# A graph-attention kernel with a fixed issue order on all engines, blocks pipelined by hand, and row merges through 32x32 turns

## The chip, the cores and the metric

The kernel runs on one core of a Trainium2 chip. The core has a matmul engine (TensorE, PE in the profile, with its weight loads shown as PEld), a vector engine (VectorE, DVE), a scalar engine (ScalarE, ACT), a general engine (GpSimd, POOL) and an engine that mostly issues transfers (SyncE, SP). Each has its own queue and works through it in order; they meet at semaphores. Matrix products land in PSUM, a small memory of eight banks; everything else lies in SBUF or in device memory (DRAM). Transfers are issued by SP, ACT and POOL and carried by 16 shared DMA engines. The metric is the device time of one execution in microseconds (us).

## The reference

A graph has 4096 nodes with 64 features each and 50,000 edges (source, destination). Four heads project the nodes, every edge gets a weight from its two ends, and each node sums its weighted incoming messages and divides by the sum of the weights:

```python
for h in range(n_heads):
    x_proj[h] = x @ weight[h]
for h in range(n_heads):
    src_att = np.sum(x_proj[h, src_nodes] * att_src[h], axis=-1)
    dst_att = np.sum(x_proj[h, dst_nodes] * att_dst[h], axis=-1)
    edge_scores[h] = src_att + dst_att
edge_scores = np.where(edge_scores > 0, edge_scores, 0.2 * edge_scores)
for h in range(n_heads):
    for i in range(num_edges):
        output[h, dst_nodes[i]] += np.exp(edge_scores[h, i]) * x_proj[h, src_nodes[i]]
# then output[h, dst] /= (sum of exp(edge_scores) over the edges into dst) + 1e-8
```

The result is 4096 x 256 (four heads of 64) in float32.

## The kernel before, in words

**Two sorts bring the edges into blocks.** Each edge becomes one float32 key that holds source group, destination and source remainder (L283 to L286). The 50,000 keys lie as 128 rows of up to 391, padded to 512 columns. `Sorter.rows` sorts every row by a bitonic network of two-operand minimum and maximum instructions (`flip` at L163 and L165, `half` at L173; two instructions on 256 elements make a step). `Sorter.runs` then merges eight neighbouring rows into a run of 4096, in three rounds: a round exchanges keys with a partner row (a stream shuffle L188, a scaling L190 and a minimum L192, once, twice and three times in rounds one to three), rescales (L194) and does nine `half` steps. `store` (L200) writes the runs to DRAM. `below` (L208) counts on ACT, by sums of signs, how many keys lie under each boundary; `bounds` (L220 to L236) turns the counts into start and end of each window, with a matmul `cnt_ps` (L220) and a dozen small DVE instructions. `fetch` (L242, L244) gathers windows out of the stored runs with indirect transfers issued by POOL. The first sort groups edges by source; its windows, two of 256 keys in every row, are the rows of the second sort (`group`), which skips the row phases that are done already and orders by destination. Its windows (five of 128 keys) are unpacked (L339 to L346) into 16-bit node numbers and written to the DRAM table `gat_bins`.

**Between the sorts' inputs and the blocks lie the tables.** `xf` (x itself, loaded at L294) is cast to bf16 into `xa` (L316), transposed on PE (L322) into `xT`, and 66 small float32 matmuls `at_ps` (L327) give the two attention terms of every node. They need `uv`, made from `wS` (the weights, L296) and `attbd` (the attention vectors).

**34 blocks of 121 destination nodes do the work.** A block has 16 tiles of 128 edges. Its node numbers are loaded to all partitions at once (`bc`, 1 MB, L363, SP and POOL taking turns). DVE makes one-hot matrices from them (`oh`, L366 and L367). PE gathers with them the source rows and scores of every edge (`xps`, 48 matmuls, L377 to L381), ACT takes the exponentials (`ex`, L384 and L385) and copies the rows out (`xs`, L386). PE also multiplies the destination one-hots by an identity to turn them (`sp`, L391) and ACT copies them out (`Sb`, L393). DVE forms the weights `wv` (L396) and the weighted rows `val` (L400); POOL copies the weights into the last four columns of `val` (L399). 16 matmuls of 260 columns scatter-add into `acc` (L405). `finish` then divides on DVE (L411 to L414), transposes `agg` on PE (L419), copies (`aT`, L420), projects with the block-diagonal weights (`pf`, L422), copies (`res`, L424) and stores (L426).

**The order.** A scheduler of the language decides the order of the instructions on each engine, and tiles with a number of buffers (`oh`: two, `bc`: three, `xps`: two of two banks, `sp`: two) decide how far ahead an engine may run.

Of the kernel before, what the change touches and what calls it, by code (L numbers as in the profile page):

```python
# [9 lines left out]
P = 128  # L10
ALPHA = 0.2
# [24 lines left out]
def kernel(ctx: ExitStack, tc: tile.TileContext, x: bass.AP, edge_index: bass.AP,  # L36
# [12 lines left out]
    XC = Din + H  # L49
# [15 lines left out]
    eD = cst.tile([P, EL, 2], I32)  # L65
    if rem:
        r0 = rem // 32 * 32
        V.memset(eS[r0:P, E0, :], N)
        V.memset(eD[r0:P, E0, :], 0)
    for t, k, eng in ((eS, 0, nc.sync), (eD, 1, nc.scalar)):  # L70
        eng.dma_start(out=t[:, 0:E0, :], in_=ei[k, 0:P * E0, :].rearrange("(p e) c -> p e c", p=P))
    for t, k, eng in ((eS, 0, nc.sync), (eD, 1, nc.scalar)):
        if rem:
            eng.dma_start(out=t[0:rem, E0, :], in_=ei[k, P * E0:E, :])
# [3 lines left out]
    G.iota(pidx[:], pattern=[[1, 1]], base=0, channel_multiplier=1)  # L78
    ident = cst.tile([P, P], F32)
    make_identity(nc, ident[:])  # L80
    io = cst.tile([P, P], I32)
    G.iota(io[:], pattern=[[1, P]], base=0, channel_multiplier=0)
    ioF = cst.tile([P, P], F32)
    V.tensor_copy(out=ioF[:], in_=io[:])
    pF = cst.tile([P, 2], F32)
    V.tensor_copy(out=pF[:, 0:1], in_=pidx[:])
    V.tensor_scalar(out=pF[:, 1:2], in0=pF[:, 0:1], scalar1=float(P), scalar2=None, op0=OP.add)

    sgi = cst.tile([P, 3], I32)
    sg = cst.tile([P, 3], F32)  # L90
    for j in range(3):
        V.tensor_scalar(out=sgi[:, j:j + 1], in0=pidx[:], scalar1=1 << j, scalar2=None, op0=OP.bitwise_and)
        V.tensor_scalar(out=sg[:, j:j + 1], in0=sgi[:, j:j + 1], scalar1=-2.0 / (1 << j), scalar2=1.0,
                        op0=OP.mult, op1=OP.add)
    sgg = cst.tile([P, 2], F32)
    V.tensor_tensor(out=sgg[:], in0=sg[:, 0:2], in1=sg[:, 1:3], op=OP.mult)
# [8 lines left out]

    p8 = bits("p8", 3, 15)
# [3 lines left out]
    m16 = cst.tile([P, 16], F32)  # L110
    V.tensor_scalar(out=m16[:], in0=ioF[:, 0:16], scalar1=p8[:, 0:1], scalar2=None, op0=OP.is_equal)
    m8 = cst.tile([P, 8], F32)
    V.tensor_scalar(out=m8[:], in0=ioF[:, 0:8], scalar1=p16[:, 0:1], scalar2=None, op0=OP.is_equal)

    sel1 = cst.tile([P, 2, P], F32)
    for i in range(2):
        V.tensor_scalar(out=sel1[:, i, :], in0=av(ioF[:], 8 * i, [0, 16], [1, 8]), scalar1=p8[:, 0:1], scalar2=None,
                        op0=OP.is_equal)
    sel2 = cst.tile([P, P], F32)
    V.tensor_scalar(out=sel2[:], in0=av(ioF[:], 0, [0, 8], [1, 16]), scalar1=p8[:, 0:1], scalar2=None,  # L120
                    op0=OP.is_equal)
    nb1 = cst.tile([P, NR + 1], F32)
    V.tensor_scalar(out=nb1[:], in0=ioF[:, 0:NR + 1], scalar1=-float(SG), scalar2=SG / 2, op0=OP.mult, op1=OP.add)
# [3 lines left out]
    V.tensor_scalar(out=nb2[:], in0=nb2[:], scalar1=0.5, scalar2=None, op0=OP.add)  # L127
    pad = cst.tile([1, W1], F32)
# [4 lines left out]
    S.copy(out=identb[:], in_=ident[:])  # L133

    xa = cst.tile([P, NB, XC], BF16)
    adb = cst.tile([P, ND, H], BF16)
# [8 lines left out]
    class Sorter:  # L145
# [13 lines left out]
        def flip(self, k):  # L159
            s, d = self.step()  # L160
            h = 1 << (k - 1)
            n = L >> k
# [5 lines left out]
        def half(self, j):  # L168
# [7 lines left out]
        def rows(self, first):  # L176
# [321 lines left out]
```

## Time and profile before

| | us |
|---|---|
| time, median of three runs | 451.8 (449.31 to 452.3) |
| profiled execution: time | 452.86 |
| profiled execution: span in the trace | 450.8 |
| last store issued | 442.7 |

| engine | busy us | instructions |
|---|---|---|
| PE | 252.3 | 3102 |
| DVE | 290.0 | 594 |
| ACT | 193.3 | 526 |
| POOL | 98.4 | 84 |

The execution falls into stretches. Up to 106 us the first sort runs on DVE; to 157 us the second; to 181 us the windows travel through DRAM; from 181 to 443 us run the 34 blocks. No engine is busy throughout, so the shares over the whole span say little: each stretch is read by itself, first by the busy time of the engines in it, then by what each engine waited for. A row of the groups by line gives the busy time and the mean of one instruction, then the idle time just before and who ended it. In a timeline row, the first two numbers are start and duration in us, and a wait stands in brackets.

### The profile page before, as it was taken

To read this page: it belongs to the slowest core of one execution; us is meant where nothing else is said; L and a number is where in the kernel's file an instruction comes from. 1 tells how busy PE (TensorE), PEld (TensorE's weight loads), DVE (VectorE), ACT (ScalarE), POOL (GpSimd) and SP (SyncE) were. 2 spreads that over 40 slices of the span, in tenths; PEclk is the share of its full clock that TensorE was granted. 3 is DMA by queue.
4 is the path that set the end of the run, shared out by engine and by line. 5 is a ranking of instruction groups with operands and counts; after the bars stand their busy time and mean duration, and the time that the engine had idled before them with its cause. 6 is when DMAs were issued, how large, how long until landed. Compare 5 with 4: busy or idle time off the path is not lost.

```text
span 450.8 us, 7963 instructions
## 1 busy us (share of the span) xinstructions
PE 252.3 (56%) x3102; PEld 212.0 (47%) x3102; DVE 290.0 (64%) x594; ACT 193.3 (43%) x526; POOL 98.4 (22%) x84
## 2 busy tenths in 40 slices
PE   0599900000000000669877887789788978797881
PEld 0388800000000000557666776667666766676660
DVE  4960199994899821755586658665876577656830
ACT  1823100000896000435556555655565556555560
POOL 6100000001000040131342124422442144314400
PEclk9999999999999999868899889998989898989897
DMA  7000000001000014923435453544345443533000
GB/s 170 7 1 0 0 0 0 1 0 37 10 0 1 7 45 151 345 95 127 182 124 201 135 183 121 201 148 166 138 178 176 140 160 155 199 117 105 23 26 17
DMA packets 13547, 43.87 MB, mean 97 GB/s; under 512 B 3308, under 2 KB 8492, under 8 KB 9148
## 3 DMA queue, kind: packets, MB, share of 16 engines
q1 hardware_dynamic: 9156, 24.16, 16.0%
q0 software_dynamic: 3152, 18.49, 11.1%
q10 hardware_dynamic: 1192, 0.63, 0.5%
q8 instruction: 26, 0.43, 0.4%
q14 instruction: 21, 0.17, 0.1%
HBM read 38.22 MB, written 5.05 MB: 96 GB/s over the span
## 4 chain that ended last, share of the span: by engine, by line
DVE 37%; PE 35%; ACT 12%; issue 6%; DMA 6%; POOL 1%; ACTq 1%; POOLq 0%; DVEq 0%; SPq 0%
PE acc L405 9%; PE sp L391 8%; DVE oh L366 7%; ACT junk L208 7%; PE at_ps L327 6%; DVE val L400 6%; PE pf L422 6%; DVE sB L173 5%; DVE sA L173 5%; DVE oh L367 3%; PE pf L419 2%; ACT aT L420 2%; DVE agg L414 2%; DMA bc<-gat_bins 2%; PE xps L377 2%
## 5 line engine op out<-in xcount | busy, mean ns | idle before, releaser
L393 ACT CAST Sb<-sp 128x512 bf16<-128x512 f32 x136 | 77.7, 591 | 46.8 <-PE sp L391 46.2
L366 DVE TENSOR_SCALAR oh<-bc,pF 128x4096 bf16<-128x4096 bf16 x34 | 43.7, 1286 | 83.1 <-PE sp L391 70.1
L405 PE MATMUL acc<-val,Sb 128*128 128x260 bf16 x544 | 88.8, 303 | 0.8 <-DVE val L400 0.8
L399 POOL COPY val<-wv 128x64 bf16<-128x64 bf16 x34 | 73.6, 2165 | 34.4 <-DVE wv L396 21.3
L400 DVE TENSOR_TENSOR val<-xs,wv 128x4096 bf16<-128x4096 bf16 x34 | 78.0, 2295 | 2.3 <-DVE wv L396 0.5
L377 PE MATMUL xps<-xa,oh 128*128 128x68 bf16 x544 | 60.2, 194 | 32.9 <-DVE oh L366 32.5
L377 PEld LDWEIGHTS <-oh 128*128 128x128 bf16 x544 | 50.2, 98 | 38.2 <-DVE oh L366 36.2
L379 PE MATMUL xps<-xa,oh 128*128 128x68 bf16 x544 | 56.9, 198 | 11.6 <-DVE oh L367 11.6
L391 PE MATMUL sp<-identb,oh 128*128 128x128 bf16 x544 | 59.4, 239 | 0.4 <-ACT res L424 0.2
L405 PEld LDWEIGHTS <-Sb 128*128 128x128 bf16 x544 | 54.1, 109 | 10.7 <-DVE val L400 0.9
L381 PE MATMUL xps<-adb,oh 128*128 128x4 bf16 x544 | 56.1, 167 | 0.0
L379 PEld LDWEIGHTS <-oh 128*128 128x128 bf16 x544 | 48.7, 96 | 15.0 <-DVE oh L367 14.8
L208 ACT ACTIVATE junk<-kr,nb 128x512 f32<-128x512 f32 x34 | 24.5, 722 | 60.8 <-DVE kr L265 59.8
L391 PEld LDWEIGHTS <-oh 128*128 128x128 bf16 x544 | 46.0, 108 | 9.8 <-issue 2.8
L381 PEld LDWEIGHTS <-oh 128*128 128x128 bf16 x544 | 50.3, 100 | 0.3
L220 PE MATMUL cnt_ps<-sgn,sel 128*128 128x17 f32 (+1 forms) x6 | 1.9, 398 | 80.9 <-ACT sgn L211 80.7
L363 POOL DMA_DIRECT2D bc<-gat_bins x17 | 9.2, 543 | 152.1 <-DVE wv L396 135.3
L384 ACT ACTIVATE ex<-xps 128x32 f32<-128x32 f32 x68 | 13.5, 199 | 67.4 <-PE xps L381 67.4
L386 ACT CAST xs<-xps 128x512 bf16<-128x512 f32 x68 | 40.3, 593 | 0.0
L220 PEld LDWEIGHTS cnt_ps<-sgn,sel 128*128 128x128 f32 x6 | 1.5, 310 | 81.3 <-ACT sgn L211 81.0
L173 DVE TENSOR_TENSOR sB<-sA 128x256 f32<-128x256 f32 x100 | 38.1, 422 | 1.5
L173 DVE TENSOR_TENSOR sA<-sB 128x256 f32<-128x256 f32 x96 | 36.6, 421 | 1.4
(119 smaller groups left out, 339.0 us busy)
## 6 DMA issues: line engine op xcount, KB each, us to landing
bc<-gat_bins SPq DMA_DIRECT2D x17, 1024.0 KB
bc<-gat_bins POOLq DMA_DIRECT2D x17, 1024.0 KB, 5.1
out_dram<-res SPq DMA_DIRECT2D x33, 121.0 KB
gat_sorted<-sA SPq DMA_DIRECT2D x2, 256.0 KB
eS<-in_edge_index_dram SPq DMA_DIRECT2D x1, 390.0 KB
eD<-in_edge_index_dram ACTq DMA_DIRECT2D x1, 390.0 KB
gat_bins<-tb SPq DMA_DIRECT2D x5, 32.0 KB
gat_bins<-tb ACTq DMA_DIRECT2D x5, 32.0 KB
```

The costliest lines, as they stand in the source:

```text
L173: V.tensor_tensor(out=av(d[:], o, [2 * h, n], [1, h]), in0=av(s[:], 0, [2 * h, n], [1, h]), in1=av(s[:], h, [2 * h, n], [1, h]), op=op)
L208: S.activation(out=junk[:], in_=v, func=ACTF.Sign, bias=nbnd[:, b:b + 1], scale=1.0, accum_out=sgn[:, b:b + 1])
L366: V.tensor_scalar(out=oh[:, 0:2, :], in0=bc[:], scalar1=pF[:, 0:1], scalar2=None, op0=OP.is_equal)
L377: T.matmul(out=o, lhsT=oh[:, 1, e], rhs=xa[:, 2 * t, :], start=(i % 4 == 0), stop=False, skip_group_check=True)
L379: T.matmul(out=o, lhsT=oh[:, 2, e], rhs=xa[:, 2 * t + 1, :], start=False, stop=False, skip_group_check=True)
L381: T.matmul(out=o[:, Din:XC], lhsT=oh[:, 0, e], rhs=adb[:, b, :], start=False, stop=True, skip_group_check=True)
L386: S.copy(out=xs[:, hf * HT:(hf + 1) * HT, :], in_=av(xps[:], 0, [512, 2], [XC, 4], [1, Din]))
L391: T.matmul(out=sp[:, i, :], lhsT=oh[:, 0, t * W2:(t + 1) * W2], rhs=identb[:], start=True, stop=True)
L393: S.copy(out=Sb[:, 4 * q:4 * q + 4, :], in_=sp[:])
L399: G.tensor_copy(out=av(val[:], C, [1, H], [CW, NT]), in_=av(wv[:], 0, [2 * NT, H], [2, NT]))
L400: V.tensor_tensor(out=av(val[:], 0, [Dout, H], [CW, NT], [1, Din]), in0=av(xs[:], 0, [0, H], [2, NT * Din // 2], [1, 2]), in1=av(wv[:], 0, ...
L405: T.matmul(out=acc[:], lhsT=Sb[:, t, :], rhs=val[:, t, :], start=(t == 0), stop=(t == NT - 1))
```

## The change

What it does, part by part:

- **Fixed order.** The whole of the main path stands under `tc.manual_schedule()`: every engine takes its instructions in the order in which the program is written. The table code moves into a function `tables`, which is called after the first sort's `store`; the loads of `xf` and `wS` (new L302 and L304) are both issued on SP. `bounds` follows `tables`, and the check of the longest run (`longest`) is split off and follows later.
- **Short columns skipped.** While rows are sorted up to length 8, only 392 of 512 columns are worked on, and 384 up to length 128.
- **Turns.** Only the first merge round uses the shuffle. In rounds two and three DVE turns 32x32 pieces (new L212), does the exchange between rows as steps within rows (`opposed`, new L192, and `half`), and turns back.
- **Constants.** Four selection masks are built on POOL rather than DVE. `below` reads the source numbers directly.
- **Blocks.** Written out as a software pipeline: in iteration b the engines get load(b+3), weigh(b), gather(b+1), turn(b+1), onehot(b+2), the end of block b-1 and scatter(b). All loads of `bc` are on SP. `xps` has one buffer of four banks. The tables hold the scores a second time, times 0.2 (72 columns where there were 68, and 8 where there were 4), so one exponential of 128 elements takes the place of four of 32 elements, and one copy `xs` of 1024 elements that of two of 512. `turn` uses PE transposes into bf16 PSUM, and ACT copies them in two pieces of 1024 instead of four of 512.
- **Scatter.** `val` is now the stationary operand and the turned one-hots `Sb` the moving one, so the sums land transposed: per tile two matmuls of 128 columns, and a third of four columns for the sum of weights. That drops the POOL copy, the transposes of `agg`, and one ACT copy; ACT copies `acc` (260 columns) to `aT`, PE projects, and DVE divides out of PSUM into `res`.

The instructions of SP up to the first loads of blocks, before (`gat_sorted` is the DRAM copy of the sorted runs):

```order
L71 DMA eS<-in_edge_index_dram 128x780
L74 DMA eS<-in_edge_index_dram 80x2
L294 DMA xf<-in_x_dram 128x32x64
L200 DMA gat_sorted<-sA 128x512 x2
L348 DMA gat_bins<-tb 8x16x128 x5
L363 DMA bc<-gat_bins 128x4096 x3
```

and now:

```order
L67 DMA eS<-in_edge_index_dram 128x780
L73 DMA eS<-in_edge_index_dram 80x2
L237 DMA gat_sorted<-sA 128x512
L302 DMA xf<-in_x_dram 128x32x64
L304 DMA wS<-in_weight_dram 64x4x64
L237 DMA gat_sorted<-sA 128x512
L362 DMA gat_bins<-tb 8x16x128 x8
L382 DMA bc<-gat_bins 128x4096 x3
L362 DMA gat_bins<-tb 8x16x128 x2
```

The load of `xf` stood ahead of the first store and now stands behind it; the load of `wS` was on ACT's queue and is behind it too.

The instructions of DVE in the first sort where the counts come in, before (`sA` and `sB` are the sorter's two buffers, `pick`, `ws` and `we` belong to `bounds`):

```order
L173 TENSOR_TENSOR sB<-sA 128x16x16 x2
L222 TENSOR_SCALAR cnt_359<-cnt_ps 128x17
L173 TENSOR_TENSOR sA<-sB 128x32x8 x2
L225 TENSOR_TENSOR pick_361<-cnt_359,m_106 128x16
L225 TENSOR_TENSOR pick_365<-cnt_359,m_106 128x16
L173 TENSOR_TENSOR sB<-sA 128x64x4 x2
L227 TENSOR_REDUCE ws_129<-pick_361 128x1
L227 TENSOR_REDUCE we_130<-pick_365 128x1
L173 TENSOR_TENSOR sA<-sB 128x128x2 x2
```

and a merge round now, with its turns (the counts come behind the last round):

```order
L212 STREAM_TRANSPOSE sA<-sB 128x512
L192 SCALAR_TENSOR_TENSOR sB<-sA 128x128x2 x2
L183 TENSOR_TENSOR sA<-sB 128x256 x2
L212 STREAM_TRANSPOSE sB<-sA 128x512
L183 TENSOR_TENSOR sA<-sB 128x256 x2
L183 TENSOR_TENSOR sB<-sA 128x2x128 x2
```

The instruction that reads the counts stood in the middle of the first sort's row phase and now stands behind the whole sort.

The instructions of DVE in the middle of the blocks, before:

```order
L366 TENSOR_SCALAR oh<-bc,pF 128x4096
L367 TENSOR_SCALAR oh<-bc,pF 128x2048
L411 TENSOR_SCALAR inv<-acc 128x4
L396 TENSOR_TENSOR wv<-ex 128x128
L412 RECIPROCAL inv<-inv 128x4
L400 TENSOR_TENSOR val<-xs,wv 128x4x16x64
L414 TENSOR_TENSOR agg<-acc,inv 128x256
L396 TENSOR_TENSOR wv<-ex 128x128
L400 TENSOR_TENSOR val<-xs,wv 128x4x16x64
L366 TENSOR_SCALAR oh<-bc,pF 128x4096
```

and now, one iteration after the other:

```order
L433 TENSOR_TENSOR wv<-ex 128x128
L437 TENSOR_TENSOR val<-xs,wv 128x4x16x64
L390 TENSOR_SCALAR oh<-bc,pF 128x4096
L391 TENSOR_SCALAR oh<-bc,pF 128x2048
L493 TENSOR_SCALAR inv<-aT 128x4
L494 RECIPROCAL inv<-inv 128x4
L496 TENSOR_TENSOR res<-pf,inv 128x256
L433 TENSOR_TENSOR wv<-ex 128x128
```

The one-hots of a block used to follow the weighted rows of the block next to it in a changing pattern; now those of block b+2 always follow `val` of block b, and the division of block b-1 comes last.

The core of the diff:

```diff
+        def opposed(self, j):
+            s, d = self.step()
+            h = 1 << j
+            n = L >> (j + 1)
+            for o, op in ((0, OP.min), (h, OP.max)):
+                V.scalar_tensor_tensor(out=av(d[:], o, [2 * h, n], [1, h]), in0=av(s[:], h, [2 * h, n], [1, h]),
+                                       scalar=-1.0, in1=av(s[:], 0, [2 * h, n], [1, h]), op0=OP.mult, op1=op)
+        def rows(self, first, n=L):
+            w8 = -(-n // 8) * 8
+            w128 = n // 128 * 128 if n % 128 <= 8 else L
             for k in range(first, 10):
-                self.flip(k)
+                w = w8 if k <= 3 else w128 if k <= 7 else L
+                self.flip(k, w)
                 for j in range(k - 2, -1, -1):
+                    self.half(j, w)
...
+            for m in range(1, 3):
+                self.turn()
+                self.opposed(m)
+                for j in range(m - 1, -1, -1):
                     self.half(j)
+                self.turn()
                 for j in range(8, -1, -1):
                     self.half(j)
...
+    def tables(pr, pps, pp1):
+        S.copy(out=identb[:], in_=ident[:])
         xf = pr.tile([P, NB, Din], F32)
         nc.sync.dma_start(out=xf[:], in_=x.rearrange("(b p) d -> p b d", p=P))
         wS = pr.tile([Din, H, Dout], F32)
-        nc.scalar.dma_start(out=wS[:], in_=weight.rearrange("h c o -> c h o"))
+        nc.sync.dma_start(out=wS[:], in_=weight.rearrange("h c o -> c h o"))
...
+            S.copy(out=to[:, :, 0:H], in_=ps[:])
+            S.mul(out=to[:, :, H:2 * H], in_=ps[:], mul=ALPHA)
...
+            for t in range(NT):
+                for k in range(2):
+                    T.matmul(out=acc[:, k * P:(k + 1) * P], lhsT=val[:, t, k * P:(k + 1) * P], rhs=Sb[:, t, :],
+                             start=(t == 0 and k == 0), stop=(t == NT - 1), skip_group_check=True)
+                T.matmul(out=acc[:, C:CW], lhsT=Sb[:, t, :], rhs=av(wv[:], 2 * t, [2 * NT, H]), start=False,
+                         stop=(t == NT - 1), skip_group_check=True)
+            self.sink.take(b, acc[:])
...
+            self.onehot(0)
+            self.gather(0)
+            self.turn(0)
+            between()
+            self.onehot(1)
+            for b in range(ND):
+                self.load(b + 3)
+                self.weigh(b)
+                self.gather(b + 1)
+                self.turn(b + 1)
+                self.onehot(b + 2)
+                if b:
+                    self.sink.give(b - 1)
+                self.scatter(b)
+            self.sink.give(ND - 1)
...
+    with tc.manual_schedule():
...
+            so.rows(1, EL)
+            store(skey1, so.runs())
+            tables(pr, pps, pp1)
+            bounds(so1, pp1, sgn, NR, EL, [sel1[:, 0, :], sel1[:, 1, :]], off1, m16, NR, ws1, we1)
...
+            group(so2, pp2, ws1[:])
+            win = Windows(cst, ws2[:])
+            longest(so2, pp2, ws1, we1, 0)
+            longest(so2, pp2, ws2, we2, 1)
...
+            blocks = Blocks(st, Finish(st))
+            for i in range(NI - 1):
+                win.unpack(i)
+            blocks.run(lambda: win.unpack(NI - 1))
```

`between` is the unpacking of the fifth window; `give` is the end of a block (projection, division, store) and `take` the copy of `acc` to `aT`.

More of the change, by code (lines that the diff above doesn't have):

```diff
@@ L109 @@
     pm8 = bits("pm8", 0, 7)
[L110 to L123, printed above, removed]
+    goff = cst.tile([P, 1], F32)
+    V.tensor_scalar(out=goff[:], in0=p8[:], scalar1=-float(SG * N), scalar2=None, op0=OP.mult)
     nb2 = cst.tile([P, ND + 1], F32)
@@ L132 @@
     identb = cst.tile([P, P], BF16)
-    S.copy(out=identb[:], in_=ident[:])
     xa = cst.tile([P, NB, XC], BF16)
-    adb = cst.tile([P, ND, H], BF16)
+    adb = cst.tile([P, ND, 2 * H], BF16)
     Wbd = cst.tile([P, 2, P], F32)
```

395 lines of the change are left out of this document (221 added, 174 removed).

## The prediction

> **What bounds the kernel now.** I read busy times by stretch first, since no engine is busy throughout.
>
> ```profile
> 29.90:54.90 25.00, 24.94 (x114) 23.39 (x113) 0.03 (x2) 5.71 (x16) 0.00 (x0) 1.00 0.00 1
> 54.90:106.40 51.50, 0.98 (x3) 0.58 (x3) 49.65 (x140) 0.00 (x0) 0.00 (x0) 1.00 0.00 0
> 113.70:156.70 43.00, 1.02 (x3) 0.58 (x3) 40.91 (x110) 27.89 (x69) 0.00 (x0) 1.00 0.00 0
> 180.90:442.70 261.80, 211.61 (x2924) 176.50 (x2924) 171.60 (x238) 146.49 (x408) 82.14 (x50) 0.91 0.41 147
> ```
>
> The columns after the stretch and its length are busy us of PE, PEld, DVE, ACT and POOL, then granted clock, DMA share and GB/s. DVE alone works in the sorts (with ACT's counts beside the second), except from 29.9 to 54.9, where it does nothing and PE everything. In the 34 blocks (7.7 us each) every engine idles for some of the time. So I ask who waited.
>
> ```profile
> DVE cnt L222 <- PE cnt_ps L220: 25.5, 2, 25.0
> DVE oh L366 <- PE sp L391: 70.1, 31, 4.2
> PE pf L419 <- DVE agg L414: 28.4, 24, 3.5
> SPq L200 <- DVE sA L173: 153.5, 2, 103.7
> ```
>
> The sort stood 25 us behind a count, whose matmul lay in PE's queue behind the tables. In the blocks DVE waits for the one-hots to be released by PE, and PE for DVE's division: two queues that block each other, no full engine. The last row matters for the change: SP stood 103.7 us at a store, in order.
>
> **The first sort.**
>
> ```profile
> 131.00 0.72 DVE L188 STREAM_SHUFFLE sZ<-sB 128x512 f32<-128x512 f32 x1
> 132.91 0.72 DVE L188 STREAM_SHUFFLE sZ<-sA 128x512 f32<-128x512 f32 x1
> 134.82 0.49 DVE L194 TENSOR_SCALAR sA<-sB,sg 128x512 f32<-128x512 f32 x1
> 135.34 0.76 DVE L173 TENSOR_TENSOR sB<-sA 128x256 f32<-128x256 f32 x2
> 136.14 0.76 DVE L173 TENSOR_TENSOR sA<-sB 128x256 f32<-128x256 f32 x2
> ...
> L173 DVE TENSOR_TENSOR sB<-sA 128x256 f32<-128x256 f32 x100 | 38.1, 422 | 1.5
> ...
> L284 DVE TENSOR_TENSOR vF<-eS,sli 128x391 f32<-128x391 int32 x1 | 0.6, 566 | 0.0
> ```
>
> A shuffle step costs 1.91 us from start to start, a rescaling 0.52, a `half` step 0.80. The wait removed: -25.0. Short columns: 566 minus 422 ns over 135 elements is 1.07 ns per element; 60 elements fewer in 2 x 6 instructions and 64 fewer in 2 x 22 save 0.8 + 3.0 = 3.8. Turns, per sort: five shuffle steps and two rescalings go (10.6); four turns, two `opposed` steps and three `half` steps come. The trace has no 32x32 turn. Its nearest rows are the rescaling (0.49) and the shuffle (0.72), both over 512 elements; I take the shuffle's, 0.75 with its gap, and twice that as the far end. An `opposed` step is two instructions like a `half`'s with a scaling, some 0.9. So 3.0 + 1.8 + 2.4 = 7.2 comes: -3.4 per sort, from -4.3 (turn at 0.49) to -0.4 (at 1.5). The masks moved to POOL and the counts moved out of the row phase free DVE of some short instructions; that I leave out of the sum as a small gain. The first store was issued at 106.42, so it comes at 106.4 - 25.0 - 3.8 - 3.4 = **74.2**.
>
> **What now stands behind that store.** On SP, the loads of `xf` and `wS` are queued behind it, and SP waits at it until 74.2. Everything of the tables on PE and ACT needs them; `cnt_ps` is queued on PE behind the tables; `bounds` on DVE needs it, POOL's fetch needs `bounds`, and the second sort the fetch. Before, the tables ran under the sort. Now nothing covers them.
>
> ```profile
> 1.83 0.88 SPq L294 DMA_DIRECT2D xf<-in_x_dram  x1
> ...
> 5.90:10.00 4.10, 0.34 (x1) 0.18 (x1) 3.92 (x11) 0.21 (x1) 1.03 (x2) 1.00 1.00 204
> ...
> 12.81 1.88 ACT L316 CAST xa<-xf 128x2048 bf16<-128x2048 f32 x1
> 16.57 1.06 PE L322 MATMUL ps<-ident,xf 128*64 128x128 f32 x4
> 43.48 10.83 PE L327 MATMUL at_ps<-uv,xT 64*128 64x4 f32 x50
> 54.23 0.61 PE L220 MATMUL cnt_ps<-sgn,sel 128*128 128x17 f32 x2
> ```
>
> Issue 0.9 behind the store's 0.3, about 2 to the first landing (the store below took 2.1), then 1 MB at 204 GB/s, about 5: data at 82. `wS` comes right behind on the same queue; `uv` takes some 2 more. From the first transpose to `cnt_ps` PE took 37.7, nearly without a gap, and the `xa` cast now stands in front of ACT's copies (1, the rest overlaps): 82 + 2 + 38 + 1 = 123. Counts and `bounds`, a chain of short instructions, 2.
>
> ```profile
> 108.57 0.17 DVE L242 CAST wi<-ws 128x2 int32<-128x2 f32 x1 [2.18 <-DMA gat_sorted<-sA]
> 113.71 0.49 DVE L265 TENSOR_SCALAR kr<-raw,goff 128x512 f32<-128x512 f32 x1 [4.97 <-DMA raw<-gat_sorted,wi]
> 156.74 0.33 SPq L200 DMA_DIRECT2D gat_sorted<-sA  x1
> 158.85 0.17 DVE L242 CAST wi<-ws 128x5 int32<-128x5 f32 x1 [2.27 <-DMA gat_sorted<-sA]
> 159.76 0.94 POOL L244 DMA_INDIRECT win<-gat_sorted,wi  x1 [47.88 <-DVE wi L242]
> 166.15 0.29 DVE L339 TENSOR_SCALAR kb<-win,boff 128x128 int32<-128x128 f32 x1 [1.04 <-DMA win<-gat_sorted,wi]
> ...
> 169.71 3.51 SPq L348 DMA_DIRECT2D gat_bins<-tb  x5
> 175.54 0.80 SPq L363 DMA_DIRECT2D bc<-gat_bins  x2
> 180.86 1.29 DVE L366 TENSOR_SCALAR oh<-bc,pF 128x4096 bf16<-128x4096 bf16 x1 [10.48 <-DMA bc<-gat_bins]
> ```
>
> The second sort starts 5.1 after `wi`: at **130**, where it was at 113.7. It took 43.0 to its store and loses 3.4 to the turns: store at 169.7, first window fetch 3.0 later, 172.7. From there it was 21.1 to the first one-hot. Now the loads of blocks stand behind four windows, not five, and a load waits only for the stores of its own window: fourth window 6.4 (159.76 to 166.15), unpacking about 1.2 (four instructions of 0.29), two issues of 0.7 (3.51 for five), the load's 5.3, together 14.3. First one-hot at **187**, which was 180.9: what the sort gains, the late tables take back. The fifth window's stores wait on SP for its unpacking, which DVE does behind the first one-hot; the load of block 3 is behind them and wanted some 10 us later.
>
> **The blocks.**
>
> ```profile
> 270.18 1.29 DVE L366 TENSOR_SCALAR oh<-bc,pF 128x4096 bf16<-128x4096 bf16 x1 [3.37 <-PE sp L391]
> ...
> 275.05 0.28 DVE L396 TENSOR_TENSOR wv<-ex 128x128 bf16<-128x128 f32 x1
> ...
> 345.57 0.17 PE L381 MATMUL xps<-adb,oh 128*128 128x4 bf16 x1
> 345.66 0.17 PE L381 MATMUL xps<-adb,oh 128*128 128x4 bf16 x1
> ...
> 342.04 0.38 PE L391 MATMUL sp<-identb,oh 128*128 128x128 bf16 x4
> 342.26 0.39 PE L405 MATMUL acc<-val,Sb 128*128 128x260 bf16 x2
> ...
> 341.46 0.69 PE L422 MATMUL pf<-Wbd,aT 128*128 128x128 f32 x4
> ...
> L386 ACT CAST xs<-xps 128x512 bf16<-128x512 f32 x68 | 40.3, 593 | 0.0
> ```
>
> DVE did all seven instructions of a block in 4.87 (270.18 to 275.05); in the new order the chains inv, reciprocal, `res` and `wv`, `val` aren't interleaved: some 0.3 more, 5.2. PE at full clock: a tile's three gather matmuls take 0.09 (345.57 to 345.66), 16 tiles 1.45, with the wider tables 1.5; a turn of 128 columns 0.055 (0.22 for four), 16 make 0.9; `pf` 0.55 net of its drain; the scatter 16 x (2 x 0.055 + 0.03) = 2.25, where 16 matmuls of 260 columns took about 0.11 each. Together 5.2. ACT: 593 ns for 512 elements is about 1.0 for 1024 (0.85 ns each); three such, `aT` 0.4 and one `ex` 0.3 make 3.7: it drops out. DMA carried 147 GB/s at a share of 0.41; 1.17 MB per block in 5.35 us would be 219 at 0.6: covered, three blocks ahead. The store of `res` stands before the next load on SP, but that load is wanted two iterations later. DVE's `val` of block b needs only ACT's copy of the iteration before, PE's scatter only that `val`, so neither engine stops the other: the period is the larger sum plus hops. I take **5.35**, against 7.7.
>
> The PE transposes into bf16 PSUM aren't in the trace. Float32 transposes are: the four of L322 above take 1.06, or 0.21 each net of the drain (421 ns), and those of `agg` 0.11:
>
> ```profile
> 340.54 0.41 PE L419 MATMUL pf<-ident,agg 128*128 128x128 f32 x2 [0.15 <-DVE agg L414]
> ...
> 442.30 0.37 ACT L424 COPY res<-pf 128x256 f32<-128x256 f32 x1 [0.84 <-PE pf L422]
> ```
>
> I take L391's 0.055, since its operands are the same two bf16 matrices; 0.11 and 0.21 are rivals.
>
> **The sum.** First one-hot 187. To `val` of block 0: one-hots 1.9, fifth window 1.2, one-hots 1.9, `wv` and `val` 2.6: 7.6. Then 33 x 5.35 = 176.5, less one pair of one-hots (1.9) that the end lacks; scatter 2.25, `aT` 0.4, projection 0.55, `res` 0.4, hops 0.6: 4.2. From the end of `res` (442.7) to the span's end was 8.1. 187 + 7.6 + 176.5 - 1.9 + 4.2 + 8.1 = 381.5 of span; the profiled execution took 452.86 for 450.8, so 383.6; it lay 1.1 above the median of 451.8: **382.5**.
>
> **The rivals.**
> 1. *Slower turns on PE (18%).* At `agg`'s 0.11 a block's PE work is 6.1, and DVE waits: 33 x 0.75 = +25, 407. A clock that stays at the 0.91 of the stretch instead makes 5.7 of 5.2, 394, within the forecast. For it: float32 transposes are the only ones seen. Against: bf16 operands.
> 2. *Much slower turns: slower than before (4%).* At L322's 0.21, 3.4 in place of 0.9, a block takes 7.7: 33 x 2.35 = +78, 460. It decides from a period of 7.45 (69 us over 33 blocks), so from 0.2 per transpose. The Trainium skill, "TensorE: Matmul & The Clock Gate", Part 4, speaks against the change: it puts a PE-mode transpose at about 275 ns in a kernel and says that transposes don't raise the clock as matmuls do. By that rule 16 of them would take 4.4, a block 8.7, and the kernel some 493. The 0.41 for two `agg` transposes, 0.11 apart, speaks against reading that figure as a pitch.
> 3. *The change doesn't hold the tables back (5%).* If the loads of x passed the store, the second sort would start at 74.2 + 7.3 = 81.5, 48 earlier: 334. Against it stands the 103.7 us wait of SP.
> 4. *Both full engines a little faster (3%)*: period 4.9, 368 or less.
>
> The forecast, 70%, spans 364 to 398: period 5.0 to 5.7, turns on DVE up to twice as long, x landing some us off. With rival 1 the range is **364 to 408**; the ends beyond hold about 2 in 10. Within 1% is what a measurement of this kernel can't tell from no change: 0.01. Faster by more 0.95, slower 0.04 (rival 2).
>
> **What would show it.** Right: DVE idle from about 74 to 122 before `cnt`, PE busy there; `kr` near 130; first one-hot near 187; then one-hots 5.3 apart, PE and DVE both over 90% busy, ACT near 70%, POOL idle, no long wait of L390. Wrong: the at_ps matmuls before the first store; `sp` matmuls more than 0.1 apart; a wait of L390 for `bc`, so that transfers bound the blocks; a turn on DVE much over 0.75.

## The result, and the profile after

The changed kernel took **373.56 us** (median of four runs, 373.35 to 374.36) against 452.05 (449.31 to 452.48) of the kernel before on the same chip: ratio **0.828**, 95% interval 0.824 to 0.831. The profiled execution took 373.68 for a span of 371.9.

The front first. These are rows of the timeline of the changed kernel, DVE, PE, SP and POOL in order of time; each has start, duration, engine, line and tile, and a wait in brackets.

```profile
72.49 0.35 SPq L237 DMA_DIRECT2D gat_sorted<-sA  x1
...
73.98 3.73 SPq L304 DMA_DIRECT2D wS<-in_weight_dram  x1
80.80 0.33 PE L318 MATMUL ps<-ident,wS 64*128 64x64 f32 x1 [80.80 <-DMA wS<-in_weight_dram]
82.74 1.92 PE L330 MATMUL ps<-ident,xf 128*64 128x128 f32 x8
...
90.00 26.68 PE L335 MATMUL at_ps<-uv,xT 64*128 64x4 f32 x132
116.60 1.03 PE L256 MATMUL cnt_ps<-sgn,sel 128*128 128x17 f32 x4
117.25 0.18 DVE L258 TENSOR_SCALAR cnt<-cnt_ps 128x17 f32<-128x17 f32 x1 [44.78 <-PE cnt_ps L256]
...
124.91 0.49 DVE L291 TENSOR_SCALAR kr<-raw,goff 128x512 f32<-128x512 f32 x1 [5.03 <-DMA raw<-gat_sorted,wi]
163.61 0.34 SPq L237 DMA_DIRECT2D gat_sorted<-sA  x1
166.38 0.94 POOL L283 DMA_INDIRECT win<-gat_sorted,wi  x1 [43.23 <-DVE mxr L272]
...
180.71 1.29 DVE L390 TENSOR_SCALAR oh<-bc,pF 128x4096 bf16<-128x4096 bf16 x1 [6.97 <-DMA bc<-gat_bins]
```

The first sort ends 34 us earlier than before (store at 72.49, before at 106.42), and then DVE stands idle for 44.78 us, because the tables run only now: their data is loaded behind the store. The first one-hot comes at 180.71, before at 180.86. The front has gained nothing, although each of its sorts is shorter.

So all of the gain lies in the blocks. The timeline of DVE over one block, and of PE's turns and projection in it:

```profile
269.85 2.29 DVE L437 TENSOR_TENSOR val<-xs,wv 128x4096 bf16<-128x4096 bf16 x1
272.06 1.28 DVE L390 TENSOR_SCALAR oh<-bc,pF 128x4096 bf16<-128x4096 bf16 x1
273.25 0.75 DVE L391 TENSOR_SCALAR oh<-bc,pF 128x2048 bf16<-128x2048 bf16 x1
273.91 0.17 DVE L493 TENSOR_SCALAR inv<-aT 128x4 f32<-128x4 f32 x1
274.11 0.18 DVE L494 RECIPROCAL inv<-inv 128x4 f32<-128x4 f32 x1
274.38 0.42 DVE L496 TENSOR_TENSOR res<-pf,inv 128x256 f32<-128x256 f32 x1
274.72 0.28 DVE L433 TENSOR_TENSOR wv<-ex 128x128 bf16<-128x128 f32 x1
275.11 2.29 DVE L437 TENSOR_TENSOR val<-xs,wv 128x4096 bf16<-128x4096 bf16 x1
```

```profile
270.60 1.05 PE L425 MATMUL sp<-identb,oh 128*128 128x128 bf16 x16
271.49 0.66 PE L490 MATMUL pf<-Wbd,aT 128*128 128x128 f32 x4
```

DVE's row has no wait in it: 5.26 us from `val` to `val`, seven instructions one behind another. PE's 16 turns take 0.89 from the first to the projection behind them, 0.056 each.

The busy times by stretch of the changed kernel (after the stretch: PE, PEld, DVE, ACT and POOL, then granted clock, DMA share, GB/s), and its chief wait (in all, times, longest):

```profile
72.50:116.60 44.10, 34.42 (x170) 31.78 (x170) 0.00 (x0) 7.41 (x15) 0.00 (x0) 0.72 0.13 32
...
186.50:357.50 171.00, 169.78 (x3803) 164.78 (x3802) 163.53 (x227) 112.72 (x166) 0.00 (x0) 1.00 0.60 215
```

```profile
DVE cnt L258 <- PE cnt_ps L256: 44.8, 1, 44.8
```

In the blocks PE is busy for 99% of the time, DVE for 96%, ACT for 66%, POOL not at all. A busy PE is not a full one: one of the turns lasts 0.22 in the profile and the next starts 0.056 after it, so durations cover gaps. The one-hots wait once, at the very start, for a load (the 6.97 above); the 70.1 us in which they waited for the turns are gone.

### The profile page after: what moved, and what is told of

Read it like the earlier page. It is cut to its first block, busy times and chain, and to the rows that moved or that the text cites. A ratio compares the mean times of both kernels' runs of the same rounds, so it can differ in the third digit from the quotient of the medians.

```text
span 371.9 us, 9662 instructions
## 1 busy us (share of the span) xinstructions
PE 215.6 (58%) x4122; PEld 206.5 (56%) x4122; DVE 282.4 (76%) x584; ACT 164.3 (44%) x290; POOL 18.9 (5%) x40
## 4 chain that ended last, share of the span: by engine, by line
DVE 60%; PE 25%; DMA 6%; issue 3%; ACT 2%; SPq 1%; POOL 1%; DVEq 0%; POOLq 0%
DVE val L437 14%; DVE sA L183 11%; DVE sB L183 10%; DVE oh L390 7%; PE at_ps L335 7%; PE acc L448 7%; DVE oh L391 4%; PE sp L425 3%; DVE res L496 3%; PE xps L403 3%; DMA wS<-in_weight_dram 2%; PE xps L405 2%; PE pf L490 1%; PE ps L330 1%; DMA bc<-gat_bins 1%
## 5 line engine op out<-in xcount | busy, mean ns | idle before, releaser
L448 PE MATMUL acc<-Sb,val 128*128 128x128 bf16 x1088 | 79.9, 217 | 1.2
L450 PE MATMUL acc<-wv,Sb 128*128 128x4 bf16 x544 | 76.0, 168 | 0.0
L448 PEld LDWEIGHTS <-val 128*128 128x128 bf16 x1088 | 67.2, 96 | 6.3 <-DVE val L437 6.1
L426 ACT COPY Sb<-sp 128x1024 bf16<-128x1024 bf16 x68 | 66.2, 1039 | 0.0
L403 PE MATMUL xps<-xa,oh 128*128 128x72 bf16 x544 | 53.9, 194 | 15.5 <-DVE oh L390 15.5
L405 PE MATMUL xps<-xa,oh 128*128 128x72 bf16 x544 | 53.7, 195 | 0.4 <-DVE oh L391 0.4
L407 PE MATMUL xps<-adb,oh 128*128 128x8 bf16 x544 | 52.8, 169 | 0.0
L183 DVE TENSOR_TENSOR sA<-sB 128x256 f32<-128x256 f32 (+2 forms) x108 | 39.7, 409 | 1.8
L183 DVE TENSOR_TENSOR sB<-sA 128x256 f32<-128x256 f32 (+2 forms) x100 | 36.8, 409 | 1.7
L425 PE MATMUL sp<-identb,oh 128*128 128x128 bf16 x544 | 36.6, 221 | 0.0
L258 DVE TENSOR_SCALAR cnt<-cnt_ps 128x17 f32<-128x17 f32 (+1 forms) x3 | 0.5, 180 | 44.8 <-PE cnt_ps L256 44.8
L412 ACT CAST xs<-xps 128x1024 bf16<-128x1024 f32 x34 | 34.2, 1007 | 0.0
```

What stands on the lines that cost most here:

```text
L183: V.tensor_tensor(out=av(d[:], o, [2 * h, n], [1, h]), in0=av(s[:], 0, [2 * h, n], [1, h]), in1=av(s[:], h, [2 * h, n], [1, h]), op=op)
L403: T.matmul(out=o, lhsT=oh[:, 1, e], rhs=xa[:, 2 * t, :], start=(t % 4 == 0), stop=False, skip_group_check=True)
L405: T.matmul(out=o, lhsT=oh[:, 2, e], rhs=xa[:, 2 * t + 1, :], start=False, stop=False, skip_group_check=True)
L407: T.matmul(out=o[:, Din:XC], lhsT=oh[:, 0, e], rhs=adb[:, b, :], start=False, stop=True, skip_group_check=True)
L412: S.copy(out=xs[:], in_=av(xps[:], 0, [512, 4], [XC, 4], [1, Din]))
L425: T.transpose(out=sp[:, i, :], in_=oh[:, 0, t * W2:(t + 1) * W2], identity=identb[:])
```

## The experiments

Unless it is said otherwise, each kernel is the changed kernel with one edit. Times are medians of four runs.

### What the front hides

**Early loads.** The loads of `xf` and `wS` move out of `tables`, ahead of the first sort's store.

```diff
+            xf = pr.tile([P, NB, Din], F32)
+            nc.sync.dma_start(out=xf[:], in_=x.rearrange("(b p) d -> p b d", p=P))
+            wS = pr.tile([Din, H, Dout], F32)
+            nc.sync.dma_start(out=wS[:], in_=weight.rearrange("h c o -> c h o"))
             so.rows(1, EL)
             store(skey1, so.runs())
-            tables(pr, pps, pp1)
+            tables(pr, pps, pp1, xf, wS)
```

> The two loads of xf and wS are issued on SP ahead of the first sort's store; everything else stays. My theory: the store held the tables back (from 73.1 to 116.6) and the tables held cnt_ps, bounds and the fetch, so the idle DVE stretch before cnt (44.8) goes; cnt follows the sort at once, kr comes near 80 in place of 124.9 and the time is 373.6 - 44.8 = 329 (325 to 334), with the blocks unchanged at 5.26 each. Rival A, the tables were not what the second sort waited for: 373. Rival B, PE, ACT or the load of x running beside the first sort slows DVE's sort steps (0.74 to 0.80 each): part of it is given back, 335 to 345.

Measured: **328.87** (328.84 to 328.91), ratio 0.728 to before, 44.7 less than the changed kernel. Two timeline rows of DVE in this kernel, and the first sort's stretch:

```profile
72.49 0.17 DVE L258 TENSOR_SCALAR cnt<-cnt_ps 128x17 f32<-128x17 f32 x1
...
80.17 0.48 DVE L291 TENSOR_SCALAR kr<-raw,goff 128x512 f32<-128x512 f32 x1 [5.05 <-DMA raw<-gat_sorted,wi]
```

```profile
20.00:72.40 52.40, 34.34 (x173) 31.43 (x173) 50.06 (x132) 10.53 (x26) 0.71 (x3) 0.65 0.00 1
```

`cnt` follows the sort at once, `kr` comes 44.7 earlier, and PE has done its 34.34 us under the sort. DVE is busy for 50.06 in this stretch; in the changed kernel, with PE at rest, it is 50.06 too. So the tables cost the sort nothing (rival B falls), and the wait was all theirs (rival A falls).

**The row merges and the short columns.** Two kernels undo one part each: the merges go back to shuffles, and the first sort's rows to 512 columns.

```diff
-            for m in range(1, 3):
-                self.turn()
-                self.opposed(m)
...
+            for m in range(1, 4):
+                for i, j in enumerate(range(m - 1, -1, -1)):
...
+                    V.stream_shuffle(out=self.z[:], in_=s[:], mask=[p ^ x_or for p in range(32)])
```

> The row merges go back to shuffles in all three rounds; everything else stays. From the rows of after (turn 0.74 pitch, opposed 0.79, half 0.80) a sort has 4 x 0.74 + 2 x 0.79 + 3 x 0.80 = 6.9 in place of 5 x 1.91 + 2 x 0.52 = 10.6, so each sort gets 3.7 longer, both on the path: 373.6 + 7.4 = 381 (380 to 382). Rival, turns cost as much as the shuffles that they replace: 373.6.

```diff
-            so.rows(1, EL)
+            so.rows(1, L)
```

> The first sort's rows go over all 512 columns; everything else stays. By 1.07 ns per element the shorter columns save 0.8 + 3.0 = 3.8: 377.4 (376.5 to 378.5). Rival, a step's time is set by a fixed part and not by its columns: 373.6 to 375.

Measured: **380.9** (380.41 to 381.93) with the old merges, +7.3; **377.16** (376.93 to 377.53) with full columns, +3.6. Both rivals fall. The groups by line of the changed kernel (count, then busy us and mean ns):

```profile
L183 DVE TENSOR_TENSOR sA<-sB 128x256 f32<-128x256 f32 x86 | 32.8, 422 | 1.5
L183 DVE TENSOR_TENSOR sA<-sB 128x192 f32<-128x192 f32 x18 | 5.7, 355 | 0.3
L212 DVE STREAM_TRANSPOSE sB<-sA 128x512 f32<-128x512 f32 x6 | 4.3, 711 | 0.2
L192 DVE SCALAR_TENSOR_TENSOR sB<-sA 128x256 f32<-128x256 f32 x4 | 1.5, 422 | 0.1
```

A turn of 512 columns takes 711 ns, like the shuffle (0.72 in the rows before) and not like the rescaling (0.49). The `opposed` step's instruction takes as long as a `half`'s, 422; its scaling is free. And 64 columns fewer save 67 ns, 1.05 per element.

### What bounds a block

**DVE longer.** The third one-hot is made twice.

```diff
                 V.tensor_scalar(out=oh[:, 2, :], in0=bc[:, 1, :], scalar1=pF[:, 1:2], scalar2=None, op0=OP.is_equal)
+                V.tensor_scalar(out=oh[:, 2, :], in0=bc[:, 1, :], scalar1=pF[:, 1:2], scalar2=None, op0=OP.is_equal)
```

> The third one-hot (0.75 on DVE) is made twice in each block. If DVE bounds the block: the period goes from 5.26 to 6.01, 373.6 + 34 x 0.75 = 399. If PE bounds it and DVE has the 0.2 to 0.4 that my sums left open: 385 to 392.

**PE longer.** Every turn is made twice.

```diff
                     T.transpose(out=sp[:, i, :], in_=oh[:, 0, t * W2:(t + 1) * W2], identity=identb[:])
+                    T.transpose(out=sp[:, i, :], in_=oh[:, 0, t * W2:(t + 1) * W2], identity=identb[:])
```

> Each of the 16 turns on PE is made twice in each block, 16 more transposes of 128x128 bf16. By their pitch of 0.055 that is 0.88. If PE is as full as DVE (busy 4.96 of 5 in the blocks): period 5.26 + 0.88 = 6.14, 403. If DVE alone bounds and PE has 0.2 to 0.3 left: 393 to 396. Rival, a transpose costs the 0.21 that its row's mean shows, or more: 16 x 0.21 = 3.4 per block, over 480.

Measured: **399.25** (398.88 to 399.69) with the longer DVE, +25.7, which is 0.76 for each of the 34 blocks, where the added instruction takes 0.75: DVE bounds the blocks, and nothing of the added instruction is hidden. With the longer PE **399.59** (399.21 to 400.31), +26.0, between the two values expected. The first and the last of PE's 32 turns in a block, from that kernel's timeline:

```profile
253.70 0.22 PE L425 MATMUL sp<-identb,oh 128*128 128x128 bf16 x1
...
255.43 0.22 PE L426 MATMUL sp<-identb,oh 128*128 128x128 bf16 x1
```

31 steps in 1.73 us: a transpose costs 0.056 and not the 0.22 that its row shows as duration. The 16 that were added make 0.89, and the period in this kernel was 5.93 (`val` of neighbouring blocks at 256.92 and 262.85), so PE's own sum in the changed kernel is 5.93 - 0.89 = 5.04. It had 0.22 per block to spare under DVE's 5.26. Of the +26.0, 31 steps of 0.67 make 20.8. The last step gives 2.5: in the changed kernel it is 3.40, since no one-hots are left to make, and here PE keeps it at 5.93. The rest are four longer steps (7.02 at the second, 6.18 to 6.87 at three late ones), whose cause is open.

```profile
256.92 2.29 DVE L438 TENSOR_TENSOR val<-xs,wv 128x4096 bf16<-128x4096 bf16 x1
262.85 2.29 DVE L438 TENSOR_TENSOR val<-xs,wv 128x4096 bf16<-128x4096 bf16 x1
```

The Trainium skill, "TensorE: Matmul & The Clock Gate", Part 4, has about 275 ns for a PE-mode transpose in a kernel; as a pitch (the time from one start to the next) that is five times what this trace shows, and as a duration it is near the 0.22. The same page of the Trainium skill, Part 1, section "Wait — 56ns, not 53.3ns?", gives 55.6 ns from start to start for matmuls of 128 columns at full clock: with that the trace agrees, for transposes too. Nor does the clock suffer: the blocks of the changed kernel are granted 1.00, with 16 transposes in each.

**DVE shorter.** `res` is made by ACT.

```diff
-            V.tensor_tensor(out=res[:], in0=av(pf[:], 0, [Dout, H], [1, Dout]), in1=av(inv[:], 0, [1, H], [0, Dout]),
-                            op=OP.mult)
+            for h in range(H):
+                S.mul(out=res[:, h, :], in_=pf[:, h * Dout:(h + 1) * Dout], mul=inv[:, h:h + 1])
```

> res is made on ACT, four copies of 64 columns scaled by the head's inverse, not on DVE (0.43). ACT had 3.1 to 3.4 of 5 busy and gets about 0.9. If DVE alone bounds: period 4.84, 373.6 - 33 x 0.42 = 360. If PE is as full: the period falls only to PE's sum, 5.1 to 5.2: 368 to 372. Rival, ACT's copies of the turns come later behind the division and hold PE: no gain or some loss.

Measured: **367.77** (367.19 to 368.9), -5.8, just under the 368 to 372 expected for a PE that is as full. Rows of its DVE timeline:

```profile
259.15 2.29 DVE L437 TENSOR_TENSOR val<-xs,wv 128x4096 bf16<-128x4096 bf16 x1
263.88 2.29 DVE L437 TENSOR_TENSOR val<-xs,wv 128x4096 bf16<-128x4096 bf16 x1
268.81 1.29 DVE L390 TENSOR_SCALAR oh<-bc,pF 128x4096 bf16<-128x4096 bf16 x1 [2.65 <-DMA bc<-gat_bins]
```

DVE alone would run at 4.73 (259.15 to 263.88), gets ahead of PE, and then stands still for 2.65: over the blocks, PE's 5.04 holds. The wait is put down to a load of `bc`; SP issues each of these behind the store of a `res`, which comes at PE's pace, as its own rows show (5.04 from one to the next):

```profile
255.97 0.33 SPq L499 DMA_DIRECT2D out_dram<-res  x1
256.39 0.33 SPq L382 DMA_DIRECT2D bc<-gat_bins  x1
261.01 0.33 SPq L499 DMA_DIRECT2D out_dram<-res  x1
```

So the wait alone does not show transfers to be the bound.

### What parted the two engines

In the kernel before, a block took 7.5 us from `val` to `val` on average (7.7 by the whole stretch), unevenly: the blocks went in pairs, two `val` 2.93 apart and then 11 to 12.5 to the next. No engine was full. Two parts of the change seemed to have ended that: the order written by hand, and the sums that come transposed. Each was undone alone, then both, and at last the writing one block ahead.

**The scheduler's order**, everything else as changed:

```diff
-    with tc.manual_schedule():
+    with ExitStack():
```

> The fixed order is taken away: the scheduler orders the same instructions (turns, transposed sums and short columns stay). It puts the loads of x ahead of the store, but cnt of the first counts back into the middle of the first sort, behind the tables on PE, as it was before the change. My theory: the 44.8 idle before cnt goes and a wait of about 24 in the sort returns (cnt_ps near 54), so the first one-hot comes about 20 earlier, near 160; in the blocks the division comes elsewhere in DVE's row and the period stays within 5.3 to 5.8: 353 to 372. Rival, the order written by hand is what frees the blocks: the period goes back towards 7.7 and the time is 353 + 33 x 2.4 = 432.

**Untransposed sums**, in the written order: the one-hots are stationary again, DVE divides ahead of the projection, and PE turns the result.

```diff
-                for k in range(2):
-                    T.matmul(out=acc[:, k * P:(k + 1) * P], lhsT=val[:, t, k * P:(k + 1) * P], rhs=Sb[:, t, :],
-                             start=(t == 0 and k == 0), stop=(t == NT - 1), skip_group_check=True)
+                T.matmul(out=acc[:, 0:C], lhsT=Sb[:, t, :], rhs=val[:, t, :], start=(t == 0), stop=(t == NT - 1),
+                         skip_group_check=True)
...
                 self.weigh(b)
+                if b:
+                    self.sink.divide(b - 1)
                 self.gather(b + 1)
                 self.turn(b + 1)
+                if b:
+                    self.sink.flip(b - 1)
                 self.onehot(b + 2)
-                if b:
-                    self.sink.give(b - 1)
                 self.scatter(b)
+                if b:
+                    self.sink.give(b - 1)
```

> The scatter has the one-hots stationary again and the sums come untransposed: the division goes to DVE before the projection, two float32 transposes come to PE and two copies to ACT; the written order keeps the blocks interleaved. My theory: the interleaving, not the orientation, made the gain. DVE's sum stays the same (one division of 256 elements for another), PE gets two float32 transposes of 0.11 and ACT one copy of 0.37 in exchange: the period goes from 5.26 to about 5.35 to 5.5, so 377 to 382. Rival, the transposed sums are what parted the engines: DVE's division before the projection brings back the crossed waits, the period goes to 6.5 or more and the time to 414 or more.

**Both undone**, the two edits together:

> Both at once: untransposed sums and the scheduler's order. It asks whether either of the two is needed for the blocks' gain, since each alone left most of it. If each alone suffices and one of them is needed, the crossed waits return without both: period near 7.7, 352 + 33 x 2.66 = 440. If neither is what parted the engines (the whole-block gather, the bf16 turns, the code written one block ahead and POOL's copy gone are then left), the period is PE's sum of 5.52 with the two float32 transposes: 352 + 33 x 0.48 + 3 of tail = 371 (368 to 376).

**Both undone and written block by block:**

```diff
             for b in range(ND):
-                self.load(b + 3)
-                self.weigh(b)
...
+                if b:
+                    self.load(b + 2)
+                self.onehot(b)
+                self.gather(b)
+                self.turn(b)
+                self.weigh(b)
+                self.scatter(b)
+                self.sink.divide(b)
+                self.sink.flip(b)
+                self.sink.give(b)
```

> As the kernel with neither (scheduler's order, untransposed sums), and each block's steps are written one after another, as before the change, not one block ahead. What is left of the change in the blocks is the whole-block gather, one exponential, the turns as bf16 transposes and POOL's copy gone. If writing a block ahead is what parted the engines, DVE's row has the division and the next one-hots behind the same block's val again, the crossed waits return and the period goes to 6.5 or more: 400 to 440. If the smaller parts did it, PE's sum of 5.52 stays the bound: 369 to 374.

Measured: scheduler's order **352.16** (348.82 to 352.49), 21.4 *less* than the changed kernel; untransposed sums **384.99** (384.9 to 386.86), +11.4; both undone **369.22** (367.88 to 370.64), still 4.3 less than the changed kernel; block by block **381.94** (379.58 to 383.38).

Only the run with both undone came out as expected. The scheduler's order is just below its range (353 to 372), with a period that got shorter, not longer. The untransposed sums are 3 above theirs (377 to 382): 7.9 are added up to the last `val` (186.59 to 365.53) and 2.8 behind it. Block by block lies between its two ranges (369 to 374 and 400 to 440), with no engine busy throughout (from 200 to 290 us PE for 85.20, DVE for 76.44) and uneven steps from `val` to `val`: 4.07 to 9.41, in a pattern of five blocks. No crossed waits of the old size came back in any of the four, where the one-hots alone had stood 70.1 for the turns. DVE's largest wait for PE in the blocks is in the last kernel:

```profile
DVE inv L484 <- PE acc L449: 16.4, 9, 3.8
```

The scheduler's order won in the front and in the blocks. Its wait for the counts, and a stretch of its blocks (columns as above):

```profile
DVE cnt L258 <- PE cnt_ps L256: 28.2, 1, 28.2
```

```profile
250.00:300.00 50.00, 50.00 (x1156) 49.88 (x1153) 48.77 (x71) 33.48 (x51) 0.00 (x0) 1.00 0.66 235
```

It starts the tables early and pays the old wait of `cnt` in the middle of the sort (28.2) in place of 44.8. In the blocks it lays the division between DVE's long instructions, so that DVE's seven fit into PE's 5.04, and PE is full.

What a block takes, from the first and last start of `val` (33 steps between them), is in one row of each kernel: before, block by block, both undone, scheduler's order, as changed.

```profile
L400 DVE TENSOR_TENSOR val<-xs,wv x34: 2284/2293/2342, 187.6 to 434.6; 128x4096 bf16<-128x4096 bf16 x34
```

```profile
L437 DVE TENSOR_TENSOR val<-xs,wv x34: 2279/2284/2293, 170.6 to 364.4; 128x4096 bf16<-128x4096 bf16 x34
```

```profile
L437 DVE TENSOR_TENSOR val<-xs,wv x34: 2282/2285/2294, 170.7 to 351.0; 128x4096 bf16<-128x4096 bf16 x34
```

```profile
L437 DVE TENSOR_TENSOR val<-xs,wv x34: 2281/2283/2293, 170.9 to 335.0; 128x4096 bf16<-128x4096 bf16 x34
```

```profile
L437 DVE TENSOR_TENSOR val<-xs,wv x34: 2291/2292/2293, 186.5 to 357.5; 128x4096 bf16<-128x4096 bf16 x34
```

That is 7.48, 5.87, 5.46, 4.97 and 5.18 per block. Read as steps: the small parts (one gather for a whole block, one exponential, bf16 transposes as turns with two copies in place of four, the weights as their own four columns without POOL's copy, all loads on SP) are worth 1.61; the code written one block ahead 0.41; the transposed sums 0.49; the order fixed by hand -0.21. The steps depend on where one starts: in the written order the transposed sums are worth 0.24 (5.42 to 5.18). The largest step is the one that I had not looked at, and it was not split further: which of the small parts carries the 1.61 stays open.

The clock has a share in it. In the blocks of the kernel before, it was granted 0.90 from the first to the last `val`, since it fell in places, as here:

```profile
336.00:339.00 3.00, 3.00 (x19) 2.26 (x18) 1.93 (x3) 1.43 (x3) 0.55 (x1) 0.50 0.15 44
```

PE's pace bears that out: four turns took 0.63 (at 336.63), against 0.38 at full clock (at 342.04). In the kernel written block by block the clock is 0.99 in the blocks. A tenth of the 247 us is 0.75 per block; my estimate from these figures is that up to 0.7 of the 1.61 went that way, less where PE was idle anyway. Which of the small parts keeps the clock up, no run tells.

### A version that beats both

**Early loads and the division on ACT together:**

> Early loads and the division on ACT together. If the two gains are independent (one in the front, one in the blocks), they add: 328.9 - 5.8 = 323 (321 to 325), with PE at its own sum of 5.04 per block. Rival: with the tables under the first sort the blocks start in another state and the gain on ACT shrinks: 326 to 329.

Measured: **324.27** (323.84 to 324.89): the gains add, but for one microsecond.

**And the projection in bf16**, with a fourth buffer for `bc`. The sums are rounded to bf16 ahead of the projection; the inverse still comes from float32. What this costs in accuracy is not measured here.

```diff
-            aT = self.fp.tile([P, CW], F32, name="aT")
-            S.copy(out=aT[:], in_=acc)
+            aT = self.fp.tile([P, C], BF16, name="aT")
+            S.copy(out=aT[:], in_=acc[:, 0:C])
+            den = self.fp.tile([P, H], F32, name="den")
+            S.copy(out=den[:], in_=acc[:, C:CW])
...
-            self.bcp = pool(name="bc", bufs=3)
+            self.bcp = pool(name="bc", bufs=4)
```

> On top of the previous kernel: the projection takes bf16 operands (the sums rounded to bf16, the inverse still from float32), and bc has a fourth buffer, so that loads run one block further ahead. The projection's pitch on PE is 0.50 per block in float32 and should be 2 x 0.055 = 0.11 in bf16: PE's sum 5.04 - 0.39 = 4.65, DVE's 4.73 then bounds: 323 - 33 x 0.31 = 313 (311 to 316). Rival: the loads of bc bound, at 1.17 MB per block: DVE waited 12.8 for them where its division was gone; then 318 to 323 and waits of the one-hots for bc.

Measured: **313.19** (312.42 to 313.21), ratio 0.695 to before (0.691 to 0.699). Rows of its DVE timeline:

```profile
203.33 2.29 DVE L435 TENSOR_TENSOR val<-xs,wv 128x4096 bf16<-128x4096 bf16 x1
...
208.05 2.29 DVE L435 TENSOR_TENSOR val<-xs,wv 128x4096 bf16<-128x4096 bf16 x1
```

4.72 per block, DVE's own sum again, with no wait for `bc` in the blocks. Taking 0.39 from PE moved the bound to DVE where PE's 5.04 and DVE's 4.73 said it would. The two edits were not tried apart: with 5.04 on PE the fourth buffer alone could not have gone below PE's sum, but whether the bf16 projection needs the fourth buffer is open.

## Why the prediction was right

The forecast was 382.5 and came out at 373.56, within its range, by its own mechanism: the wait in the sort gone, the tables held behind the store, the front about even, and blocks in which DVE and PE are both nearly full. Step by step, from the rows above (the last `val` starts at 357.47 and takes 2.29, the last `res` ends at 363.81):

```profile
357.47 2.29 DVE L437 TENSOR_TENSOR val<-xs,wv 128x4096 bf16<-128x4096 bf16 x1
...
363.39 0.42 DVE L496 TENSOR_TENSOR res<-pf,inv 128x256 f32<-128x256 f32 x1 [0.39 <-PE pf L490]
```

| step | predicted | measured |
|---|---|---|
| first store | 74.2 | 72.49 |
| loads of the tables there (measured: `wS`, the last) | 82 | 80.80 |
| from there to the counts' `cnt` | 41 | 36.5 |
| second sort starts (`kr`) | 130 | 124.91 |
| `kr` to the second store | 39.7 | 38.7 |
| fetch to the first one-hot | 14.3 | 14.3 |
| first one-hot | 187 | 180.71 |
| to the end of `val` of block 0 | 7.6 | 8.0 |
| from there to the end of the last `val` | 174.6 | 171.0 |
| tail to the last `res`, and behind it | 4.2 + 8.1 | 4.1 + 8.1 |

The 9.6 us between the sum (381.5) and the span (371.9) are 6.3 of front and 3.6 of blocks, with 0.3 the other way at the ends.

- **The tables were the term furthest off**: 38 from the first transpose of x to `cnt_ps`, measured 33.9 (82.74 to 116.60). I took the time over whole from before, where ACT had the counts to do beside its copies and PE's transposes of x were spread over the stretch. Now the 32 transposes are done by 90.00, and 132 `at_ps` matmuls take 0.202 each, in place of 0.217 (50 in 10.83); the last section shows their pace. Of the 1.0 us that I added for the `xa` cast, 0.68 came: PE waited that long for the first `xT`.
- **The sorts**: the turns at 0.75 were right (0.74 from start to start, quoted duration 711 ns); the `opposed` step was taken at 0.9 and costs 0.79. Undone, both sorts together lose 7.3, where I had 6.8. The short columns were taken at 3.8 and are worth 3.6.
- **The period**: 5.2 for DVE and 5.2 for PE, with 0.15 of hops, against 5.26 and 5.04. The bound is DVE alone, and its row needs no hop, since the order leaves 0.22 of PE as a cushion. My PE terms (1.5, 0.9, 0.55, 2.25) were each rounded up; the 0.3 that I gave DVE for its uninterleaved chains should have been 0.39 (4.87 to 5.26).
- **The rivals**: slow transposes (18% and 4%) fell at once, at 0.056 each, and the clock in the blocks was 1.00, not 0.91. That the tables might not be held back fell too, and the early loads put a price to it: 328.87, where I had 334. Both engines a little faster (3%) did not come either: DVE's 5.26 held the period above 4.9.
- **What was read wrongly**: the prediction takes the new order, in which `val` needs only ACT's copy of the iteration before, as what frees the two queues that block each other. The period came out right, since it was summed from engine times. But undoing the written order, the transposed sums, or both left blocks of 5.0 to 5.5 us and not 7.5, and writing the code one block ahead is worth 0.41 of the 2.3 gained. That the engines' sums would be reached was right; the reason given for it carries the smaller part, so on that point the right number does not bear it out. Whether the change needed its fixed order for the gain could not be told from the period, and the answer is that the order cost 21 us: 15.6 in the front (first one-hot at 165.12 by the scheduler, 180.71 by hand) and some 7 in the blocks, with 1 the other way behind the last `val`.

```profile
165.12 1.28 DVE L390 TENSOR_SCALAR oh<-bc,pF 128x4096 bf16<-128x4096 bf16 x1 [6.46 <-DMA bc<-gat_bins]
```

## What to carry to other kernels

When an order is written by hand, follow each queue past its first long wait: two loads written behind a store on SP cost 44.7 us here, more than half as much as the 78.5 that the whole change gained, and moving them ahead of the sort gave it back. A period summed engine by engine, from start-to-start times and not from durations, tells which engine is next and by how much (5.26, 5.04, 4.73 here), and three cheap runs that lengthen or shorten one engine confirmed it here to within 0.05 us. And a right total does not show its causes: undo the parts one by one before crediting any of them.

## What the runs showed of the hardware that was not expected

**A busy PE was slowed all the same.** The `at_ps` matmuls (float32, four columns) keep PE busy without a gap. Stretches of the kernel with early loads, in which nothing else runs on PE:

```profile
33.00:35.00 2.00, 2.00 (x20) 2.00 (x19) 1.93 (x6) 0.00 (x0) 0.00 (x0) 1.00 0.00 0
35.00:37.00 2.00, 2.00 (x14) 2.00 (x14) 1.90 (x6) 0.00 (x0) 0.00 (x0) 0.68 0.03 8
...
39.00:43.00 4.00, 4.00 (x21) 4.00 (x20) 3.82 (x11) 0.06 (x1) 0.00 (x0) 0.50 0.00 0
```

20 of them start in 2 us at a granted clock of 1.00, and then, with no pause, 21 in 4 us at 0.50: 0.10 and 0.19 each. Such matmuls are busy time in the profile, but they did not hold the clock, while the blocks' matmuls held it at 1.00; whether it is the four columns or the float32 that lets it fall, no run parts. In the changed kernel the clock falls in the tables too (0.72 over 72.50 to 116.60), so most of the 26.68 us of `at_ps` ran at half pace, in the stretch that all else waits for.

**And the recorded clock doesn't always show it.** In the kernel with the scheduler's order, a timeline row and a stretch of the same matmuls:

```profile
45.85 10.83 PE L335 MATMUL at_ps<-uv,xT 64*128 64x4 f32 x50
```

```profile
50.00:54.00 4.00, 4.00 (x21) 4.00 (x20) 0.00 (x0) 0.00 (x0) 0.00 (x0) 1.00 0.00 0
```

0.217 each, the slow pace, at a recorded 1.00; and in the kernel before it was the same 10.83 for 50, also at 1.00. Nor is the lower record the longer time: of this kernel's four executions, one has a mean recorded clock of 0.790 and took 348.82, the others 0.990 to 0.993 and 352.15 to 352.49. Which of the two, the pace or the record, is to be believed about the clock there is left open; a time is better taken from starts than from the clock.

**Engines beside each other.** DVE's sort steps took the same 50.06 us of a stretch of 52.4 with PE and ACT at work beside it as without.
